# The unit of the largest and smallest expert on quarters of the partitions, with 32 slots of each

## The chip, the cores and the metric

The kernel runs on one core of a Trainium2 chip. The metric is the device time in microseconds; three runs of the kernel before gave 1936.6, 1944.35 and 1945.28 us.

## The reference, cut to what matters

A backbone of two layers over 256 latent tokens (and 256 context tokens) of width 1024, all in float32. Each layer is a mixer of four head groups and then a channel mixer: a dense SwiGLU in layer 0, and in layer 1, where only the latent tokens are left, eight experts of which each token uses two. The change lies in that last part:

```
def _swiglu(h, w_gate, w_up, w_down):
    return (jax.nn.silu(h @ w_gate) * (h @ w_up)) @ w_down
...
    top_val, top_idx = lax.top_k(logits, TOP_K)
    top_w = jax.nn.softmax(top_val, -1)
    gate = jnp.sum(jax.nn.one_hot(top_idx, N_EXPERTS, dtype=F32) * top_w[..., None], axis=-2)
    out = jnp.zeros(h.shape, F32)
    for e in range(N_EXPERTS):
        out = out + gate[..., e:e + 1] * _swiglu(h, w_gate[e], w_up[e], w_down[e]).astype(F32)
```

An expert has an inner width of 3584 (`D_FFE`) and three matrices of 1024 x 3584, so the eight together hold 352 MB, and each is read once. 256 tokens with two experts each fill 512 places.

## The kernel before, in words

Everything ahead of line 1404 (the parameters, both mixers, the dense SwiGLU, the routing logits) is the same in both kernels, apart from a few places where the scheduler swaps neighbours. `moe()` is the expert stage.

**Ranks, slots, units.** The experts are ranked by their number of tokens while the program runs; rank 0 has the most. `CAPS` gives each rank a number of slots (192 for rank 0, then 128, 128 and five times 64), `BASE` its first slot. 128 slots make a unit, one row of the partitions each. `UNITS` names the ranks of each unit: unit 0 holds 128 slots of rank 0, units 2 and 3 ranks 1 and 2, units 4 and 5 two ranks of 64 slots each, and unit 1 the last 64 slots of rank 0 beside the 64 of rank 7, the smallest. Units of one rank (0, 2, 3) are "whole". A token that finds no slot would be computed by `overflow`, a branch of which the body runs only if there is such a token.

**Two kinds of arithmetic.** A whole unit splits each half of a weight tile (ScalarE L1571, VectorE L1572) into two float32r parts, in `whl`, four buffers in turn, and multiplies each piece in three full-array matmuls (L1595, L1596, L1598). A unit of two ranks uses plain float32 (L1608): two matmuls of 64 array columns side by side, one on partitions 0 to 63 with one expert's weights, one on 64 to 127 with the other's, both over 512 moving columns. A float32 matmul is two instructions in the trace.

**Blocks and pairs.** The inner width goes in seven blocks of 512 (`NB`). In a block a rank has six weight pieces of 1 MB: gate 0 and 1, up 2 and 3, down 4 and 5; 48 pieces a block, 336 in all. They go into a ring of nine tiles (`mw`, line 1507; loads at L1660), in the order of first use; SyncE issues a load when the tile's last reader is done. The units are worked in pairs: `PAIRS` = (1, 0), (5, 2), (4, 3), that is with the ranks {0, 7}, {5, 6, 1} and {3, 4, 2}. Block 0 has the order (5), (4), (1, 0), (2, 3), with the gather of the tokens between; the last block has (1, 0), (5, 2), (3), (4). `swiglu_units` emits for a pair: gate of the first unit (8 k-steps), gate of the second, up of both, then Silu, product, transposes (L1630) and the down step (8 k-steps for two halves of 512 outputs) of each unit. `chain` keeps the matmuls in that order. The results are weighted and added into `yacc` by VectorE (L1744). After block 3 comes `overflow` (L1673), where all engines pass the branch and the loads in flight land first.

**The end.** After block 5 POOL multiplies each `yacc` by `gate`, a row broadcast to all partitions (`bcast_rows`, L431, at line 1755), and the last block's parts are multiplied by it on VectorE (L1747) before they are added (L1748). `combine` (L1713) sends each unit's `yacc` back to its tokens by a matmul with `DT`; unit 4's is L1771. A layer norm and the output follow.

Of the kernel before, what the change touches and what calls it, by code (L numbers as in the profile page):

```python
# [47 lines left out]
def _consts():  # L48
# [32 lines left out]
    put("iota", np.tile(np.arange(NSLOT), (P, 1)))  # L81
# [112 lines left out]
def kernel(ctx: ExitStack, tc: tile.TileContext, A, out: bass.AP):  # L194
# [1209 lines left out]
    def moe():  # L1404
# [108 lines left out]
        xg, yacc, gsl = {}, {}, tab(NU)  # L1513
        DT = mp.tile([P, NU, 256], F32R, name="DT")
        xgt = mp.tile([P, NU - len(WHOLE), KT, P], F32, name="xg")
        xhl = mp.tile([P, len(WHOLE), 2, KT, P], F32R, name="xhl")
        for u in range(NU):
            n = sum(v < u for v in WHOLE)
            xg[u] = (xhl[:, n, 0], xhl[:, n, 1]) if u in WHOLE else xgt[:, u - n]

        def gather(us):
# [35 lines left out]
            for j, u in enumerate(us):  # L1557
# [23 lines left out]
        def swiglu_units(units, nk):  # L1581
# [5 lines left out]
            def step(o, x, w, ws, a0, ks, nks, n=n):  # L1587

                if isinstance(x, tuple):
# [13 lines left out]
                for a, b, w_, pos_ in halves:  # L1603
# [13 lines left out]
            for i in range(2):  # L1617
                o2[i] = [ps("mm") for _ in units]
                for (xs, ws), o in zip(units, o2[i]):
                    for h in range(2):  # L1620
                        ms = step(o, xs, 2 * i + h, ws, 4 * h, range(4 * h, 4 * h + 4), KT)
                    chain[:] = ms
            ys = [[ps("mm" if u else "s5") for _ in range(2)] for u in range(len(units))]
            for u, (xs, ws) in enumerate(units):
                h = wtile("mh")[:, :n]
                S.activation(h, o2[0][u][:, :n], AF.Silu)  # L1626
                V.tensor_mul(h, h, o2[1][u][:, :n])  # L1627
                tp = ps("tr")
                for i in range(nk):
# [94 lines left out]
        for at, (b, us) in enumerate(order):  # L1724
# [155 lines left out]
```

## Time and profile before

| | us |
|---|---|
| median of three runs | 1944.35 |
| the profiled execution, its own time | 1943.62 |
| its span (first to last instruction) | 1941.8 |
| TensorE matmuls busy | 1810.1 |
| VectorE busy | 1071.2 |
| ScalarE busy | 693.1 |
| mean granted TensorE clock | 0.967 |

Times in the profile are in microseconds from the start of the span, unless marked ns. PE is TensorE's matmuls, PEld its weight loads, DVE VectorE, ACT ScalarE, POOL GpSimd, SP SyncE, which issues all DMAs. Spans of matmuls overlap, since their ends are modelled with the pipeline's depth; the distance between starts is what one costs. In a group of instructions the two numbers are the busy time of all and the mean of one in ns, then the idle time of the engine just before them with what ended it. The expert stage runs from about 1000 us to the end.

### The profile page before, as it was taken

Reading aid. Unit: us, or ns where it says so; the run is one execution under the profiler, and the core shown is the slowest. Engines: PE = TensorE matmul, PEld = TensorE weight load, DVE = VectorE, ACT = ScalarE, POOL = GpSimd, SP = SyncE. Lnnn points to the kernel's source line nnn. Section 1 sums busy time; section 2 is a strip of 40 time slices with the busy share of each in tenths; the row PEclk is TensorE's granted clock in tenths of the full one; section 3 lists DMA queues with packets and bytes.
Section 4 is the critical chain, followed back from the end, with each engine's and each line's share of the span. In section 5 each row is a group of like instructions: output and inputs, shape, how many; then the busy total and the mean of one; then the engine's idle time right before and its main releaser. Section 6 shows DMA issues by size and latency. Waiting matters only on the chain.

```text
span 1941.8 us, 23723 instructions
## 1 busy us (share of the span) xinstructions
PE 1810.1 (93%) x8634; PEld 1150.1 (59%) x8634; DVE 1071.2 (55%) x1715; ACT 693.1 (36%) x1077; POOL 420.8 (22%) x368
## 2 busy tenths in 40 slices
PE   6799989799999999899969999999999899999997
PEld 2576547778777777586654475554554454544553
DVE  7978544825456244849673383453543444554473
ACT  2245553422212222436623363342333333423340
POOL 3852232634342422522340000000000000021000
PEclk9899989899999999998979999999999999999999
DMA  8455831224534545251349987999999999999893
GB/s 315 151 164 195 290 133 65 102 95 144 187 133 165 177 172 190 76 188 52 122 164 371 417 333 324 423 420 407 422 400 422 369 379 421 409 398 421 349 378 133
DMA packets 111498, 508.57 MB, mean 262 GB/s; under 512 B 21776, under 2 KB 31632, under 8 KB 68368
## 3 DMA queue, kind: packets, MB, share of 16 engines
q1 hardware_dynamic: 111376, 507.01, 67.1%
q8 instruction: 69, 1.13, 0.2%
q14 instruction: 53, 0.43, 0.1%
HBM read 491.29 MB, written 15.66 MB: 261 GB/s over the span
## 4 chain that ended last, share of the span: by engine, by line
PE 79%; DVE 12%; DMA 3%; issue 2%; POOL 2%; ACT 1%; SPq 1%; DVEq 0%; POOLq 0%; ACTq 0%
PE ps L1608 24%; PE ps L283 8%; PE ps L284 8%; PE ps L285 8%; PE ps L1595 6%; PE ps L1598 6%; PE ps L1596 6%; PE ps L358 2%; PE ps L1096 1%; PE ps L1058 1%; PE ps L1057 1%; PE ps L1630 1%; DMA ring<-in_ada_w_dram 1%; PE ps L1114 1%; PE ps L1713 1%
## 5 line engine op out<-in xcount | busy, mean ns | idle before, releaser
L1572 DVE TENSOR_TENSOR whl<-ring,whl 128x1024 fp32r<-128x1024 f32 x252 | 307.3, 1254 | 114.3 <-ACT whl L1571 105.2
L1571 ACT ACTIVATE whl<-ring 128x1024 fp32r<-128x1024 f32 x252 | 258.0, 1054 | 234.9 <-PE ps L1596 128.8
L1608 PE MATMUL ps<-ring,xg 128*64 128x512 f32 x1344 | 302.2, 599 | 6.0 <-DMA ring<-in_moe_w_dram 6.0
L303 ACT ACTIVATE ring<-ring 128x1024 fp32r<-128x1024 f32 x114 | 120.0, 1059 | 312.7 <-PE ps L284 155.9
L283 PE MATMUL ps<-xa,ring 128*128 128x512 f32 (+1 forms) x576 | 217.2, 378 | 9.0 <-DVE xa L423 8.1
L285 PE MATMUL ps<-xa,ring 128*128 128x512 f32 (+1 forms) x576 | 216.7, 377 | 0.0
L284 PE MATMUL ps<-xb,ring 128*128 128x512 f32 (+1 forms) x576 | 216.2, 376 | 0.3 <-DVE xb L424 0.3
L1608 PEld LDWEIGHTS ps<-ring,xg 128*64 128x64 f32 x1344 | 94.6, 137 | 189.4 <-issue 186.4
L1750 POOL TENSOR_TENSOR yacc<-yacc,gate 128x1024 f32<-128x1024 f32 x6 | 21.1, 3512 | 766.9 <-DVE yacc L1744 734.9
L1608 PE MATMUL ps<-ring,mhT 128*64 128x512 f32 x672 | 161.8, 596 | 1.4 <-ACT mhT L1635 1.4
L305 DVE TENSOR_TENSOR ring<-ring,ring 128x1024 fp32r<-128x1024 f32 x76 | 106.0, 1397 | 90.9 <-ACT ring L303 90.5
L305 POOL TENSOR_TENSOR ring<-ring,ring 128x1024 fp32r<-128x1024 f32 x38 | 95.7, 2518 | 240.5 <-ACT ring L303 212.5
L1595 PE MATMUL ps<-whl,xhl 128*128 128x512 f32 x336 | 135.2, 402 | 0.0
L283 PEld LDWEIGHTS ps<-xa,ring 128*128 128x128 f32 x576 | 110.5, 192 | 36.1 <-DVE xa L423 8.5
L1596 PE MATMUL ps<-whl,xhl 128*128 128x512 f32 x336 | 131.2, 391 | 0.0
L1627 DVE TENSOR_TENSOR mh<-mh,ps 128x512 f32<-128x512 f32 x42 | 28.9, 687 | 185.3 <-PE ps L1608 159.9
L285 PEld LDWEIGHTS ps<-xa,ring 128*128 128x128 f32 x576 | 110.5, 192 | 24.4 <-issue 6.6
L284 PEld LDWEIGHTS ps<-xb,ring 128*128 128x128 f32 x576 | 110.3, 192 | 20.7 <-issue 2.8
L1598 PE MATMUL ps<-whl,xhl 128*128 128x512 f32 x336 | 104.2, 391 | 0.0
L1608 PEld LDWEIGHTS ps<-ring,mhT 128*64 128x64 f32 x672 | 48.4, 137 | 92.9 <-issue 90.6
L1744 DVE SCALAR_TENSOR_TENSOR yacc<-ps,mtab,yacc 128x512 f32<-128x512 f32 x60 | 45.0, 750 | 90.7 <-PE ps L1608 65.8
L1626 ACT ACTIVATE mh<-ps 128x512 f32<-128x512 f32 x42 | 25.0, 595 | 181.2 <-PE ps L1608 122.5
(445 smaller groups left out, 3026.6 us busy)
## 6 DMA issues: line engine op xcount, KB each, us to landing
ring<-in_moe_w_dram SPq DMA_DIRECT2D x334, 1024.0 KB, 10.5
ring<-in_ada_w_dram SPq DMA_DIRECT2D x96, 512.0 KB, 5.7
ring<-in_ffn_gu_dram SPq DMA_DIRECT2D x44, 512.0 KB, 3.5
ring<-in_w_in_dram SPq DMA_DIRECT2D x32, 512.0 KB, 4.7
ring<-in_ffn_d_dram SPq DMA_DIRECT2D x22, 512.0 KB, 3.8
ring<-in_w_out_dram SPq DMA_DIRECT2D x16, 512.0 KB, 3.9
s5CT<-CT SPq DMA_DIRECT2D x8, 512.0 KB, 3.4
s5WB<-WB SPq DMA_DIRECT2D x8, 512.0 KB, 3.0
```

Of the source, the lines that this page charges most:

```text
L283: PE.matmul(o, a[0], b[0], start=start, stop=False)
L284: PE.matmul(o, a[0], b[1], start=False, stop=False)
L285: PE.matmul(o, a[1], b[0], start=False, stop=stop)
L303: S.activation(hi, r, AF.Copy)
L305: (G if cnt[0] % 3 == 0 else V).tensor_sub(lo, r, hi.bitcast(F32))
L1571: S.activation(t[:, 0], src, AF.Copy)
L1572: V.tensor_sub(t[:, 1], src, t[:, 0].bitcast(F32))
L1595: PE.matmul(o[:, :n], xh[:, k], wh[:, k - k0], start=k == 0, stop=False)
L1596: PE.matmul(o[:, :n], xl[:, k], wh[:, k - k0], start=False, stop=False)
L1598: m = PE.matmul(o[:, :n], xh[:, k], wl[:, k - k0], start=False, stop=k == nks - 1)
L1608: PE.matmul(o[a:b, :n], x[:, k, a:b], w_(w)[:, k - a0], start=k == 0, stop=k == nks - 1, tile_position=pos_)
L1744: V.scalar_tensor_tensor(d, y[hf], g, d, op0=ALU.mult, op1=ALU.add)
```

## The change

Rank 0 gets 160 slots and rank 7 gets 32. Unit 1 now has four quarters of 32 partitions: the first two hold the same 32 slots of rank 0, the last two the same 32 slots of rank 7 (`SLOTS` repeats them, so that the gather puts each token there twice). The even quarter of an expert multiplies the first half of a weight piece's columns, the odd one the second half. A k-step is then four matmuls of 32 array columns and 256 moving columns, each at its own column position, where it was two of 64 and 512. The gate and up results of unit 1 are 256 wide, its `h` takes two transposes, and its `y` and `yacc` are 512 wide, with different output columns on even and odd quarters; so `DT` has a second version for it (`par` masks the even or the odd quarters), `combine` has two matmuls of 256 columns for it, and the gate row a rearranged copy, `gateq`. `gate` is made in the last block instead of early in the stage, POOL's products with it are gone, and the last block's parts are added first and multiplied after. `overflow` makes its own gate row, for which it passes five ring tiles over, not four. The hi and lo parts of the whole units' tokens get one tile each.

```
-CAPS = (192, 128, 128, 64, 64, 64, 64, 64)
-BASE = (0, 256, 384, 512, 576, 640, 704, 192)
+CAPS = (160, 128, 128, 64, 64, 64, 64, 32)
+BASE = (0, 256, 384, 512, 576, 640, 704, 160)
...
-UNITS = ((0, 0), (0, 7), (1, 1), (2, 2), (3, 4), (5, 6))
+UNITS = ((0, 0), (0, 0, 7, 7), (1, 1), (2, 2), (3, 4), (5, 6))
+NU = len(UNITS)
+QUART = {u for u, rk in enumerate(UNITS) if len(rk) == 4}
...
+SLOTS = np.arange(NU * P)
+SLOTS[P : 2 * P] = P + np.repeat([0, 0, 32, 32], 32) + np.tile(np.arange(32), 4)
...
+                if u in QUART:
+                    for i, v in enumerate((u, NU)):
+                        V.tensor_scalar(DT[:, v], tp[:, 0:256], C("par")[:, i : i + 1], None, op0=ALU.mult)
+                else:
+                    V.tensor_copy(DT[:, u], tp[:, 0:256])
...
-                halves = [(0, 128, ws[0], None)] if ws[0] is ws[1] else [
-                    (64 * a, 64 * a + 64, ws[a], (0, 64 * a)) for a in range(2)
-                ]
+                if len(ws) == 2 and ws[0] is ws[1]:
+                    parts = [(0, 128, ws[0], None, slice(0, n))]
+                else:
+                    z = 128 // len(ws)
+                    parts = [
+                        (z * a, z * a + z, w_, (0, z * a), slice(n * (a % 2), n * (a % 2) + n) if z == 32 else slice(0, n))
+                        for a, w_ in enumerate(ws)
+                    ]
...
                             PE.matmul(
-                                o[a:b, :n], x[:, k, a:b], w_(w)[:, k - a0], start=k == 0, stop=k == nks - 1, tile_position=pos_
+                                o[a:b, :n], x(k, a) if callable(x) else x[:, k, a:b], w_(w)[:, k - a0, c],
+                                start=k == 0, stop=k == nks - 1, tile_position=pos_,
                             )
-                            for a, b, w_, pos_ in halves
+                            for a, b, w_, pos_, c in parts
...
+                        for c, v, d in ((0, u, 256), (256, NU, 512)) if u in QUART else ((0, u, 512),):
+                            y = yacc[u][:, 256 * h : 256 * h + 256] if u in QUART else yacc[u][:, 512 * h : 512 * h + 512]
...
+            if (b, us) == (NB - 1, PAIRS[0]):
+                gate = mp.tile([P, D], F32, name="gate")
+                bcast_rows(gate, adaT[1][:, 40:48, 0])
+
+                gateq = mp.tile([P, 512], F32, name="gateq")
+                for a in range(4):
+                    r = slice(32 * a, 32 * a + 32)
+                    G.tensor_copy(
...
-                    elif b < NB - 1:
+                    else:
                         V.scalar_tensor_tensor(d, y[hf], g, d, op0=ALU.mult, op1=ALU.add)
-                    else:
-                        yg = wtile("mh")
-                        V.tensor_mul(yg, y[hf], gate[:, c])
-                        V.scalar_tensor_tensor(d, yg, g, d, op0=ALU.mult, op1=ALU.add)
-                if b == NB - 2:
-                    G.tensor_mul(yacc[u], yacc[u], gate)
+                    if b == NB - 1:
+                        V.tensor_mul(d, d, gt[:, c])
...
-                overflow([mw() for _ in range(4)])
+                overflow([mw() for _ in range(5)])
```

TensorE's row in block 1, at the transposes and the down step of pair (1, 0). `ring_7751` and so on are the weight tiles, `mh` and `mhT` unit 1's product and its transpose, `hTl` unit 0's. Before:

```order
L1598 MATMUL ps_8789<-whl_7761,xhl 128x512 x2
L1630 MATMUL ps_8848<-small,mh_7674 128x128 x4
L1608 MATMUL ps_8842<-ring_7751,mhT_7675 64x512
L1608 MATMUL ps_8842<-ring_7752,mhT_7675 64x512
...
L1608 MATMUL ps_8843<-ring_7753,mhT_7675 64x512
L1608 MATMUL ps_8843<-ring_7754,mhT_7675 64x512
...
L1630 MATMUL ps_8876<-small,mh_7673 128x128 x4
L1595 MATMUL ps_8844<-whl_7758,hTl_7763 128x512
```

The same place in the changed kernel, where "x2" joins the two quarters that read one weight tile:

```order
L1607 MATMUL ps_8839<-whl_7761,xhl_7766 128x512 x2
L1648 MATMUL ps_8913<-small,mh_7674 128x128 x2
L1622 MATMUL ps_8908<-ring_7751,mhT_7675 32x256 x2
L1622 MATMUL ps_8908<-ring_7752,mhT_7675 32x256 x2
...
L1648 MATMUL ps_8955<-small,mh_7673 128x128 x4
L1622 MATMUL ps_8908<-ring_7753,mhT_7675 32x256 x2
L1622 MATMUL ps_8908<-ring_7754,mhT_7675 32x256 x2
...
L1604 MATMUL ps_8909<-whl_7758,hTl_7763 128x512
```

Unit 1's matmuls stand where they stood, twice as many and a quarter of the size each; unit 0's transposes have moved ahead of unit 1's second down piece.

VectorE's row at the end of pair (1, 0) in the last block, before (`yacc_8070` is unit 1's, `yacc_8060` unit 0's):

```order
L1572 TENSOR_TENSOR hTl_7762<-ps_12784,hTl_7762 128x512
L1747 TENSOR_TENSOR mh_7674<-ps_12750,gate 128x512
L1748 SCALAR_TENSOR_TENSOR yacc_8070<-mh_7674,mtab,yacc_8070 128x512
L1747 TENSOR_TENSOR mh_7673<-ps_12751,gate 128x512
L1748 SCALAR_TENSOR_TENSOR yacc_8070<-mh_7673,mtab,yacc_8070 128x512
...
L1748 SCALAR_TENSOR_TENSOR yacc_8060<-mh_7673,mtab,yacc_8060 128x512
L1572 TENSOR_TENSOR whl_7758<-ring_7751,whl_7758 128x1024
```

And in the changed kernel, with `yacc_8073` for unit 1 and `yacc_8062` for unit 0:

```order
L1581 TENSOR_TENSOR hTl_7762<-ps_13089,hTl_7762 128x512
L1784 SCALAR_TENSOR_TENSOR yacc_8073<-ps_13042,mtab,yacc_8073 128x512
L1784 SCALAR_TENSOR_TENSOR yacc_8062<-ps_13043,mtab,yacc_8062 128x512
L1786 TENSOR_TENSOR yacc_8062<-yacc_8062,gate 128x512
...
L1786 TENSOR_TENSOR yacc_8073<-yacc_8073,gateq 128x512
L1581 TENSOR_TENSOR whl_7758<-ring_7752,whl_7758 128x1024
```

Unit 1's sum comes first, its product with `gateq` last, behind unit 0's, and the next pair's split of the weights stands behind that.

## Rows read from the trace of the kernel before

**Rows 1.** The page's first part: busy time, share of the span, instructions.

```profile
PE 1810.1 (93%) x8634; PEld 1150.1 (59%) x8634; DVE 1071.2 (55%) x1715; ACT 693.1 (36%) x1077; POOL 420.8 (22%) x368
```

**Rows 2.** Stretches: length, busy PE, PEld, DVE, ACT, POOL, then clock, DMA share, GB/s.

```profile
1002.00:1055.00 53.00, 46.18 (x248) 27.30 (x249) 26.04 (x90) 14.47 (x33) 3.25 (x3) 0.88 1.00 399
1055.00:1075.00 20.00, 18.43 (x101) 8.28 (x101) 7.21 (x20) 7.91 (x18) 0.00 (x0) 1.00 0.84 331
1110.00:1215.00 105.00, 102.22 (x454) 63.22 (x452) 60.73 (x61) 49.45 (x53) 0.00 (x0) 1.00 0.85 334
...
1510.00:1540.00 30.00, 24.01 (x96) 11.43 (x96) 14.38 (x15) 8.61 (x9) 0.00 (x0) 0.89 0.85 336
1550.00:1590.00 40.00, 39.66 (x180) 20.97 (x178) 15.75 (x17) 12.72 (x15) 0.00 (x0) 1.00 0.89 369
1590.00:1680.00 90.00, 86.52 (x379) 44.18 (x376) 43.05 (x43) 30.98 (x35) 0.00 (x0) 1.00 1.01 421
1680.00:1710.00 30.00, 29.66 (x135) 16.74 (x134) 15.72 (x14) 9.71 (x11) 5.67 (x2) 1.00 0.88 362
1710.00:1790.00 80.00, 73.19 (x317) 36.37 (x317) 42.72 (x38) 27.47 (x31) 11.99 (x4) 1.00 1.01 422
1790.00:1840.00 50.00, 49.66 (x224) 26.74 (x222) 23.02 (x25) 16.39 (x19) 3.41 (x1) 1.00 0.86 350
```

**Rows 3.** DMA issues, 1001 to 1935 us: count, KB each, median us to landing.

```profile
ring<-in_moe_w_dram SPq DMA_DIRECT2D x334, 1024.0 KB, 10.5
ring<-in_moe_w_dram SPq DMA_DIRECT2D x4, 512.0 KB, 7.0
fd<-ntab SPq DMA_DIRECT2D x2, 512.0 KB, 11.1
```

**Rows 4.** Timeline of SyncE: start, us, what; the first loads of the stage.

```profile
1001.68 8.63 SPq L1660 DMA_DIRECT2D ring<-in_moe_w_dram  x9
```

**Rows 5.** SyncE's longest wait in total, 1000 to 1942 us: us, times, longest.

```profile
SPq L1660 <- PE ps L1608: 448.1, 140, 10.4
```

**Rows 6.** The chain, 1155 to 1285 us: start, us, what; the pairs of block 1.

```profile
1159.22 7.02 PE ps L1608 x32
...
1200.24 7.02 PE ps L1608 x32
...
1280.82 4.43 PE ps L1608 x18
```

**Rows 7.** Timeline of PE: unit 1 and unit 2 begin in block 0.

```profile
1081.10 7.04 PE L1608 MATMUL ps<-ring,xg 128*64 128x512 f32 x32
...
1123.37 0.47 PE L1595 MATMUL ps<-whl,xhl 128*128 128x512 f32 x1
```

**Rows 8.** Timeline of PE: quarters of 32 columns, in both layers.

```profile
84.89 1.02 PE L709 MATMUL ps<-tabx,tabs 128*32 128x240 f32 x16
...
610.36 0.61 PE L709 MATMUL ps<-tabx,tabs 128*32 128x240 f32 x8
```

**Rows 9.** Groups by line, 1000 to 1942 us: busy us, mean ns, idle before.

```profile
L1608 PE MATMUL ps<-ring,xg 128*64 128x512 f32 x1344 | 302.2, 599 | 6.0 <-DMA ring<-in_moe_w_dram 6.0
L1608 PE MATMUL ps<-ring,mhT 128*64 128x512 f32 x672 | 161.8, 596 | 1.4 <-ACT mhT L1635 1.4
L1750 POOL TENSOR_TENSOR yacc<-yacc,gate 128x1024 f32<-128x1024 f32 x6 | 21.1, 3512 | 766.9 <-DVE yacc L1744 734.9 <-DMA ring<-in_moe_w_dram 32.0
L431 PE MATMUL ps<-small 128*128 128x128 f32 x16 | 2.4, 281 | 0.0
```

**Rows 10.** Timeline of PE: the first matmuls after the branch, their wait in brackets.

```profile
1532.80 3.68 PE L1608 MATMUL ps<-ring,xg 128*64 128x512 f32 x8 [5.99 <-DMA ring<-in_moe_w_dram]
```

**Rows 11.** Timeline of PE: unit 5's last down step, and what follows it.

```profile
1854.50 7.08 PE L1608 MATMUL ps<-ring,mhT 128*64 128x512 f32 x30
1862.46 0.47 PE L1595 MATMUL ps<-whl,hTl 128*128 128x512 f32 x1 [0.88 <-DVE mh L1747]
```

**Rows 12.** The 20 us around the wait of rows 10, columns as in rows 2.

```profile
1520.00:1540.00 20.00, 14.01 (x53) 7.07 (x52) 10.20 (x10) 4.51 (x5) 0.00 (x0) 0.83 0.97 374
```

More of the change, by code (lines that the diff above doesn't have):

```diff
@@ L1512, in moe @@
         iota = C("iota")
-        xg, yacc, gsl = {}, {}, tab(NU)
-        DT = mp.tile([P, NU, 256], F32R, name="DT")
+        xg, yacc, gsl, gate, gateq = {}, {}, tab(NU), None, None
+        DT = mp.tile([P, NU + 1, 256], F32R, name="DT")
         xgt = mp.tile([P, NU - len(WHOLE), KT, P], F32, name="xg")
-        xhl = mp.tile([P, len(WHOLE), 2, KT, P], F32R, name="xhl")
+        xhl = [mp.tile([P, 2, KT, P], F32R, name=nm("xhl")) for _ in WHOLE]
         for u in range(NU):
             n = sum(v < u for v in WHOLE)
-            xg[u] = (xhl[:, n, 0], xhl[:, n, 1]) if u in WHOLE else xgt[:, u - n]
+            xg[u] = (xhl[n][:, 0], xhl[n][:, 1]) if u in WHOLE else xgt[:, u - n]
         def gather(us):
@@ L1620, in swiglu_units @@
                     for h in range(2):
-                        ms = step(o, xs, 2 * i + h, ws, 4 * h, range(4 * h, 4 * h + 4), KT)
+                        ms = step(o, xs, 2 * i + h, ws, 4 * h, range(4 * h, 4 * h + 4), KT, 2 * n // len(ws))
                     chain[:] = ms
-            ys = [[ps("mm" if u else "s5") for _ in range(2)] for u in range(len(units))]
+            ys = [
+                [ps("mm" if u else "s5") for _ in range(4 // len(ws))] for u, (_, ws) in enumerate(units)
+            ]
             for u, (xs, ws) in enumerate(units):
-                h = wtile("mh")[:, :n]
-                S.activation(h, o2[0][u][:, :n], AF.Silu)
-                V.tensor_mul(h, h, o2[1][u][:, :n])
+                m = 2 * n // len(ws)
+                h = wtile("mh")[:, :m]
+                S.activation(h, o2[0][u][:, :m], AF.Silu)
+                V.tensor_mul(h, h, o2[1][u][:, :m])
                 tp = ps("tr")
-                for i in range(nk):
+                for i in range(m // 128):
                     PE.transpose(tp[:, 128 * i : 128 * i + 128], h[:, 128 * i : 128 * i + 128], ident)
@@ L1707, in combine @@
         def combine(units):
+            units = sorted(units, key=lambda u: u in QUART)
             for h in range(2):
@@ L1712, in combine @@
                     for u in units:
-                        PE.matmul(
-                            o, DT[:, u, 128 * t : 128 * t + 128].bitcast(F32), yacc[u][:, 512 * h : 512 * h + 512],
-                            start=u == units[0], stop=u == units[-1],
-                        )
+                        for c, v, d in ((0, u, 256), (256, NU, 512)) if u in QUART else ((0, u, 512),):
+                            y = yacc[u][:, 256 * h : 256 * h + 256] if u in QUART else yacc[u][:, 512 * h : 512 * h + 512]
+                            PE.matmul(
+                                o[:, c:d], DT[:, v, 128 * t : 128 * t + 128].bitcast(F32), y,
+                                start=u == units[0], stop=u == units[-1] and d == 512,
+                            )
                     z = res[t + 2][:, 512 * h : 512 * h + 512]
```

37 lines of the change are left out of this document (21 added, 16 removed).

## The prediction

> **What bounds the kernel now.** The page's first part comes first: TensorE is busy for 93% of the span [rows 1]. That alone says "PE-bound", and would make every PE saving a saving of time, so the next view is the busy time by stretch of the expert stage, for the column GB/s and not for PE [rows 2]. It runs at 421 GB/s with a DMA share of 1.01 for stretches of 80 and 90 us; no row passes 422. 338 loads bring 336 tiles of 1 MB, 352.3 MB [rows 3], and at 421 GB/s these alone take 837 us, from the first issue at 1001.7 us [rows 4] to 1838.5 us at best. So the stage has two limits that lie close together. Between the full stretches are short ones of 362, 369, 350 or 334 GB/s, in which PE is busy for 97 to 99% [rows 2]. What happens in those is in SyncE's waits: it stands 140 times, 448 us in all, in front of a ring tile that L1608 still reads [rows 5].
>
> A tile costs the DMA 1.0486 MB / 421 GB/s = 2.49 us. Pair (1,0) reads two experts, 12 tiles, 29.9 us; pairs (5,2) and (4,3) read three, 18 tiles, 44.8 us. On PE the three cost about the same: the chain has unit 1 of block 1 beginning at 1159.2, the next pair at 1200.2 and block 2 at 1280.8 [rows 6], so 41.0 us for (1,0) and 40.3 us for each other pair. In (1,0) PE is 11 us slower than the loads, the nine-tile ring fills and the loads stop; in the other two PE is 4.5 us faster each and comes to wait for tiles. A block takes 121.6 us there, 119.6 us of it being the time of its 48 tiles: the two limits take turns, and neither hides the other whole.
>
> **The change, part by part.** *Quarters.* A k-step of unit 1 is now two half-array matmuls of 512 columns; 8 steps take 7.04 us [rows 7], 0.88 us each. It becomes four of 32 array columns and 256 moving columns. The nearest row is L709, four quarters of 240 columns: 16 instructions in 1.02 us, 8 in 0.61 us [rows 8], so 0.205 us for four; for 256 columns 0.219 us, and a step (two instructions to a float32 matmul) 0.44 us. With 24 steps a block this saves 24 x 0.44 = 10.6 us a block, 74 us of the 302 + 162 us of L1608 [rows 9]. Bounds: nothing saved (quarters one after another in pairs) up to the 10.6 us.
>
> The same row bears on a rule that speaks against the change. L709 keeps four quarters side by side at the price of one. The Trainium skill (TensorE: Matmul & The Clock Gate, Measured speedup vs the span model) reports 2.38-fold for three column tiles of 32. By that rate, an estimate from that page, four would give 3.2-fold, a step 0.55 us, a saving of 8 us a block and an end some 2 us later; the trace does not agree, and I go by L709.
>
> *What that does to a block.* Pair (1,0) falls from 41.0 to 30.4 us, level with its 29.9 us of loads, and no pair is slower on PE than on the DMA any more: 111 us a block against 119.6. So from here the loads set the pace, and most of the 74 us turns into waiting on PE. What is left to win is what the loads lose now.
>
> A second rule would leave nothing to win. The rows show 421 GB/s [rows 2]. The Trainium skill (DMA: Bandwidth & Descriptors, Where 436 GB/s comes from) puts a core's HBM loads at about 358 GB/s; by that the 352.3 MB would take 984 us, longer than the stage is. The trace disagrees, so the rule has no share in the sum.
>
> *The loads' lost time.* Lost is length x (1 - rate/421), by [rows 2]. At the start 53 x (1 - 399/421) = 2.8 and 20 x (1 - 331/421) = 4.3 us: gathers and unit 5, unchanged, kept. From 1110 to 1215, 21.7 us: pairs (1,0) and (2,3) of block 0 and (1,0) of block 1 take 42.3, 35.8 and 41.0 us on PE [rows 6, 7] against 29.9 each, an excess of 29 us of which the ring swallows some 7. After it the excess is 42.3 - 10.6 - 2.4 (L431 of line 1755, which moves away [rows 9]) - 29.9 = -0.6, then 5.9, then 0.5: 6 us, which the ring can swallow; I keep 3 (bounds 0 and 6). At line 1673 the loads drain, 30 x (1 - 336/421) = 6.1 us, and PE stands idle for 6 us [rows 2, 10]: kept, with one more ring tile passed over. The branch itself stays untaken: the reference's own router on its inputs gives the experts 137, 103, 67, 59, 44, 43, 39 and 20 tokens, within 160 and 32. At (1,0) in blocks 4, 5 and 6: 4.9, 4.2 and 8.4 us, gone.
>
> *The rest.* Unit 1's Silu, product, transposes and accumulate halve, and a second D costs one product in the gather: none is on the path. The gate's broadcast (2.4 us of PE) now lies in the last block's pair (1,0), where PE waits for loads. POOL loses six products of 3.5 us [rows 9] and gets four copies for gateq, each at most half of such a product, 7 us in all at most; their user, VectorE's product on unit 1's yacc, stands behind unit 0's down matmuls of some 6 us in its queue. I take 0, and 1 us as the upper bound; the next pair's splits are queued behind it. In combine, two matmuls of 256 columns replace one of 512: 0. VectorE's two operations for each half of y change places: 0.
>
> **The sum.** The end hangs on unit 5's down step in the last block, since from its end at 1861.6 us to the span's end at 1941.8 PE has work without a pause over 0.9 us, apart from the closing normalization [rows 11]: 80.2 us, kept. That step needs tile 316 of 336. Tiles: 316 x 1.0486 + 1.05 MB (the tokens spilled for the overflow [rows 3]) = 332.4 MB, at 421 GB/s 789.6 us. First issue 1001.7 + 789.6 + losses 7.1 + 3 + 6.1 = 1807.5 us; the tile's own matmuls 3.5 us: 1811.0 us. With the tail 1891.2 us. I add 2 us for waits on PE after which its clock is granted at half (below): span 1893. The profiled run's time is 1943.6 for a span of 1941.8, 1.8 more, and lies 0.7 below the median of 1944.35. So **1895 us**, 2.5% less. Of 74 us saved on PE, some 49 us arrive. Bounds: no loss in block 0 and no added 2 us, 1890, and 1883 if the 7.1 us at the start went too; above, 6 us in block 0, 1 us for gateq and 3 us lost at each of five pairs (1,0), since the ring holds tiles that PE lags behind on, 1914.
>
> **Rivals.** *The ring still fills at (1,0).* PE ends a pair some 6 us after its last tile, and a tile is held until split and multiplied; if that lag keeps the loads waiting for half of what they lose now (half of 21.7 + 17.5, 20 us), 1915 us. For: in blocks 4 to 6 the stalls are there though PE waits for tiles elsewhere. Against: stretches of 80 and 90 us without any stall, with the same lag [rows 2].
>
> *Quarters run in pairs.* Then the change doesn't do what it says: PE as before, plus what the broadcast adds, 1944 us. For: nothing in the expert stage. Against: L709.
>
> *PE alone sets the pace.* Then all 74 us arrive: 1870 us. Against: 837 us of loads, and no row over 422 GB/s.
>
> *The clock falls, slower than before.* PE will wait for tiles in every block. After the 6 us that it stood at the branch the granted clock of the 20 us there was 0.83 [rows 10, 12]: a drop from 2.4 to 1.2 GHz, with 6.8 us at the lower level (0.17 x 20 x 2), which costs 3.4 us of PE work. PE's reserve is 119.6 - 111 = 8.6 us a block; up to two drops a block cost little, and it decides against the change from some five a block (17 us, 8.4 over the reserve, 59 us in seven blocks). With eight: 1895 + 7 x (27.2 - 8.6) = 2025 us. Against: I find one wait of about 3.3 us a block, when unit 1 has used its first two tiles and the next two land 5 us later, and stretches with PE at 92% keep a clock of 1.00 (the last but one of [rows 2]).
>
> **How the numbers follow.** Forecast 1895: 0.83. Ring 1915: 0.07. Pairs 1944: 0.04. PE alone 1870: 0.02. Clock 2025: 0.04. The range of 1882 to 1918 covers the forecast's bounds and the ring, and leaves out some 0.1 to 0.15. A measurement of this kernel tells 0.5% (10 us) from no change: faster by more 0.92, within 0.04, slower 0.04.
>
> **What will show it.** Unit 1's eight k-steps in 3.5 us, not 7.0, with four starts together: the quarters. Pair (1,0) at about 30 us, a block at 119 to 121 us, 420 GB/s through 1110 to 1800 but for the branch, SyncE's waits on L1608 far shorter and PE's on tiles or splits longer: the loads as the pace. A granted clock under 1.00 within blocks would speak for the last rival; rates under 400 GB/s at (1,0) for the first. Wrong it is if the block stays at 122 us or more, or if the tail after unit 5's last down step is not about 80 us.

## The result, and the profile after

The changed kernel takes **1891.22 us** (median; 1889.33 to 1896.53), the kernel before, timed beside it, 1944.16 us: a ratio of 0.974, 95% interval 0.9709 to 0.9772. That is 2.7% less; 1895 was predicted, 1882 to 1918. The profiled execution took 1891.42 us for a span of 1889.6 us.

The page's first part, as [rows 1], shows almost nothing of it. TensorE is as busy as before, 93%:

```profile
PE 1748.1 (93%) x9300; PEld 1146.3 (61%) x9300; DVE 1055.4 (56%) x1708; ACT 687.5 (36%) x1076; POOL 402.7 (21%) x366
```

The stretches of the expert stage do show it (columns as in [rows 2]; the first two are of the same lengths as there, counted from this trace's own first load at 997.8 us). Between 1110 and 1800 us the last column is the same everywhere except around the branch: the short rows of 334, 369, 362 and 350 GB/s are gone from the blocks. Only the last row, in the last block, shows the loads held up by the ring's readers again.

```profile
998.00:1051.00 53.00, 45.96 (x269) 28.42 (x269) 28.24 (x96) 16.64 (x38) 3.48 (x3) 0.90 0.99 402
1051.00:1071.00 20.00, 18.43 (x92) 6.73 (x93) 5.53 (x16) 6.31 (x14) 0.00 (x0) 1.00 0.95 369
1110.00:1215.00 105.00, 101.39 (x592) 65.59 (x592) 64.08 (x65) 48.96 (x55) 0.00 (x0) 1.00 1.01 421
1215.00:1475.00 260.00, 247.32 (x1336) 136.59 (x1333) 119.65 (x119) 93.04 (x107) 0.00 (x0) 0.99 1.01 421
1475.00:1510.00 35.00, 26.12 (x148) 13.84 (x147) 15.88 (x17) 10.13 (x13) 0.00 (x0) 0.85 0.85 347
1510.00:1590.00 80.00, 78.59 (x442) 44.75 (x442) 37.11 (x37) 28.91 (x33) 0.00 (x0) 1.00 1.01 421
...
1710.00:1790.00 80.00, 75.53 (x472) 43.99 (x470) 39.02 (x40) 29.19 (x34) 2.43 (x4) 1.00 1.01 421
...
1810.00:1850.00 40.00, 38.70 (x149) 26.00 (x149) 30.64 (x34) 13.70 (x14) 0.00 (x0) 1.00 0.85 350
```

PE's timeline gives the pairs, answering [rows 6, 7, 11] (L1622 is the old L1608). The lines are the first matmuls of: (1,0), (5,2) and (4,3) of block 1, block 2, block 3, block 6; then, in block 6, unit 1's wait for a tile, its up step, and last unit 5's last down step.

```profile
1141.58 3.66 PE L1622 MATMUL ps<-ring,xg 128*32 128x256 f32 x64
...
1170.87 1.51 PE L1622 MATMUL ps<-ring,xg 128*64 128x512 f32 x6
...
1212.97 1.51 PE L1622 MATMUL ps<-ring,xg 128*64 128x512 f32 x6
...
1253.96 2.41 PE L1622 MATMUL ps<-ring,xg 128*32 128x256 f32 x36
...
1372.55 1.98 PE L1622 MATMUL ps<-ring,xg 128*32 128x256 f32 x32
...
1739.34 2.35 PE L1622 MATMUL ps<-ring,xg 128*32 128x256 f32 x36
1743.20 1.92 PE L1622 MATMUL ps<-ring,xg 128*32 128x256 f32 x28 [1.50 <-DMA ring<-in_moe_w_dram]
1750.72 4.34 PE L1622 MATMUL ps<-ring,xg 128*32 128x256 f32 x64
...
1801.37 7.08 PE L1622 MATMUL ps<-ring,mhT 128*64 128x512 f32 x30
```

The first line is the quarters: 64 instructions, eight k-steps, in 3.66 us, against 7.02 for 32 half-array instructions; the starts of four quarters lie within 0.02 us of each other. Pair (1,0) falls from 41.0 to 29.3 us. Block 1 takes 112.4 us, PE's own length (the loads had gained a lead by then: tile 50, the block's second, landed at 1132.5 us, 9 us before its first matmul); block 2 takes 118.6 us, about the loads' length.

The groups by line, 1000 to 1890 us, as [rows 9]; the last two are the copies for gateq and the late broadcast:

```profile
L1622 PE MATMUL ps<-ring,xg 128*64 128x512 f32 (+1 forms) x1792 | 270.4, 498 | 19.5 <-DMA ring<-in_moe_w_dram 17.0 <-issue 2.2
L1622 PE MATMUL ps<-ring,mhT 128*64 128x512 f32 (+1 forms) x896 | 138.7, 489 | 3.5 <-ACT mhT L1653 3.5
...
L1772 POOL COPY gateq<-gate 32x512 f32<-32x512 f32 x4 | 2.4, 607 | 765.6 <-ACT gate L440 765.5
L436 PE MATMUL ps<-small 128*128 128x128 f32 x16 | 2.2, 281 | 0.0
```

Busy time in L1622 fell by 31.8 + 23.1 = 55 us, not 74: part of the waiting counts as busy. Eight k-steps of quarters take 4.34 us at 1750.72, not 3.66, and no idle time is marked in them. Idle time on tiles rose from 6.0 to 17.0 us.

The waits, 1000 to 1890 us (engine, line, released by: us, times, longest), as [rows 5]; SyncE's two, then ScalarE's splits, which waited 88.6 us, 24 times, before:

```profile
SPq L1684 <- PE ps L1622: 352.7, 136, 12.2
SPq L1684 <- DVE whl L1581: 232.6, 111, 4.8
...
ACT whl L1580 <- DMA ring<-in_moe_w_dram: 234.0, 60, 12.5
```

And the DMA issues, as [rows 3]:

```profile
ring<-in_moe_w_dram SPq DMA_DIRECT2D x334, 1024.0 KB, 15.8
```

From issue to landing now takes 15.8 us, not 10.5. At 2.49 us a tile that is some six tiles in the queue: SyncE still stands in front of a ring tile, but the DMA behind it has work. SyncE's wait is therefore no sign of a lost load; the GB/s column is.

### The profile page after: what moved, and what is told of

It is laid out like the page before. It is cut to its first block, busy times and chain, and to the rows that moved or that the text cites. A ratio compares the mean times of both kernels' runs of the same rounds, so it can differ in the third digit from the quotient of the medians.

```text
span 1889.6 us, 24989 instructions
## 1 busy us (share of the span) xinstructions
PE 1748.1 (93%) x9300; PEld 1146.3 (61%) x9300; DVE 1055.4 (56%) x1708; ACT 687.5 (36%) x1076; POOL 402.7 (21%) x366
## 4 chain that ended last, share of the span: by engine, by line
PE 71%; DVE 13%; DMA 12%; issue 2%; ACT 2%; POOL 1%; SPq 0%; DVEq 0%; ACTq 0%; POOLq 0%
PE ps L1622 16%; DMA ring<-in_moe_w_dram 11%; PE ps L288 9%; PE ps L290 9%; PE ps L289 9%; PE ps L1604 5%; PE ps L1607 5%; PE ps L1605 5%; PE ps L363 3%; PE ps L1063 1%; PE ps L1062 1%; PE ps L1101 1%; PE ps L1119 1%; DVE ring L310 1%; PE ps L1648 1%
## 5 line engine op out<-in xcount | busy, mean ns | idle before, releaser
L1581 DVE TENSOR_TENSOR whl<-ring,whl 128x1024 fp32r<-128x1024 f32 x252 | 299.1, 1221 | 165.4 <-ACT whl L1580 156.3
L1622 PE MATMUL ps<-ring,xg 128*64 128x512 f32 (+1 forms) x1792 | 270.4, 498 | 19.5 <-DMA ring<-in_moe_w_dram 17.0
L288 PE MATMUL ps<-xa,ring 128*128 128x512 f32 (+1 forms) x576 | 217.0, 378 | 10.5 <-DVE xa L428 8.2
L1622 PEld LDWEIGHTS ps<-ring,xg 128*64 128x64 f32 (+1 forms) x1792 | 96.7, 125 | 174.4 <-issue 132.7
L1622 PE MATMUL ps<-ring,mhT 128*64 128x512 f32 (+1 forms) x896 | 138.7, 489 | 3.5 <-ACT mhT L1653 3.5
L1784 DVE SCALAR_TENSOR_TENSOR yacc<-ps,mtab,yacc 128x512 f32<-128x512 f32 x66 | 49.5, 750 | 93.6 <-PE ps L1622 60.9
L1645 DVE TENSOR_TENSOR mh<-mh,ps 128x512 f32<-128x512 f32 (+1 forms) x42 | 27.0, 642 | 131.2 <-PE ps L1622 106.4
L1622 PEld LDWEIGHTS ps<-ring,mhT 128*64 128x64 f32 (+1 forms) x896 | 46.7, 123 | 76.2 <-issue 61.4
L363 PE MATMUL ps<-ring,small 128*32 128x512 f32 x384 | 74.4, 665 | 12.3 <-ACT small L340 6.5
## 6 DMA issues: line engine op xcount, KB each, us to landing
ring<-in_moe_w_dram SPq DMA_DIRECT2D x334, 1024.0 KB, 15.8
```

Source lines behind the costliest of these rows:

```text
L288: PE.matmul(o, a[0], b[0], start=start, stop=False)
L363: PE.matmul(o[32 * j : 32 * j + 32, :], act[:, k, :], w[:, i, :], start=h < 2, stop=h >= 2, tile_position=(0, 32 * j),)
L1581: V.tensor_sub(t[:, 1], src, t[:, 0].bitcast(F32))
L1622: PE.matmul(o[a:b, :n], x(k, a) if callable(x) else x[:, k, a:b], w_(w)[:, k - a0, c], start=k == 0, stop=k == nks - 1, tile_position=pos_,)
```

## Where the 52 us came from

Three marks divide each trace: the first load's issue (I), the first matmul of block 1 (B1) and of block 6 (B6), and the span's end. The table gives I and then the three lengths, all from the timelines of the profiled executions, with the median time beside them. The experiments that keep the order of the pairs in blocks 0 to 5 stand in it too, and are told below. Differences in the text are of unrounded times.

| kernel | I | I to B1 | B1 to B6 | B6 to end | time, median |
|---|---|---|---|---|---|
| before | 1001.7 | 157.5 | 627.6 | 155.1 | 1944.2 |
| after | 997.8 | 143.8 | 597.8 | 150.3 | 1891.2 |
| before_half1 | 1004.1 | 146.8 | 601.0 | 145.7 | 1899.6 |
| before_half5 | 1005.4 | 151.5 | 609.2 | 148.2 | 1909.8 |
| after_half5 | 1002.6 | 141.5 | 599.5 | 147.2 | 1892.9 |
| before_gate | 1003.2 | 154.4 | 623.2 | 157.0 | 1938.3 |
| before_less | 996.0 | 152.1 | 620.7 | 152.5 | 1926.2 |
| after_less | 1001.9 | 139.5 | 574.5 | 150.2 | 1866.8 |
| after_ring7 | 1000.6 | 150.2 | 603.4 | 153.1 | 1905.3 |
| after_last | 1005.5 | 144.4 | 597.3 | 156.3 | 1905.2 |

Of the 52.2 us between the two spans, 3.8 lie ahead of the first load, 13.7 before block 1, 29.8 in blocks 1 to 5 and 4.8 in the last block. The 3.8 us can't be put down to the change: I lies between 996.0 and 1005.4 in the traces of the kernel before and its four variants here, and between 997.8 and 1005.5 in those of after and its four. That is a spread of some 10 us with the same work ahead of it; how much of it belongs to the execution and how much to the order in which a build puts that work is open. The lengths behind I are the surer measure.

## The experiments

**Is PE's time in unit 1 enough?** before_half1 takes only unit 1's columns, no quarters (`cut` is set for unit 1 alone):

```diff
                 for k in ks:
+                    c = slice(0, 256 if cut and k else n)
                     with behind(*chain):
...
-                                o[a:b, :n], x[:, k, a:b], w_(w)[:, k - a0], start=k == 0, ...
+                                o[a:b, c], x[:, k, a:b], w_(w)[:, k - a0, c], start=k == 0, ...
```

> The kernel before, with only half of unit 1's matmuls in time: every k-step of unit 1 but the first of its chain multiplies 256 of the 512 columns (left out: the other 256 columns of these k-steps, and with them the right numbers of unit 1). No quarters, no moved gate, no other tables. Saved on PE: 20 of 24 k-steps of a block, 0.44 us each, 8.8 us a block, 62 us in seven blocks; pair (1,0) falls from 41.0 to 32.2 us against 29.9 us of loads, the block from 121.6 to 112.8 us on PE against 119.6 us of loads. Theory (the loads set the pace as soon as (1,0) no longer lags): blocks of 119 to 121 us, rates of 420 GB/s through (1,0), time 1893 to 1903 us, close to the changed kernel's 1891 although PE has 12 us more to do. Rival 1 (PE sets the pace): 1944 - 62 = 1882 us. Rival 2 (the quarters as such, or the moved gate, bring the gain): above 1915 us.

Measured 1899.58 us, ratio 0.9781 (0.9755 to 0.9807). The theory's range holds it, and neither rival's does. From B1 to B6 it needs 601.0 us against after's 597.8, with 1.8 us a block more for PE: quarters as such aren't needed, only less time on PE. The profiled run began its loads 6.2 us later than after's, which is most of the 8 us between the two spans.

**Does the place matter?** before_half5 is the same cut with unit 5 in place of unit 1.

> The kernel before, with the same 8.8 us a block taken from unit 5 in pair (5,2) instead of unit 1 in (1,0): every k-step of unit 5 but the first of its chain multiplies 256 of 512 columns (left out: the other 256 columns of them). PE has as little to do as in the run that halves unit 1, but (1,0) still takes 41.0 us against 29.9 us of loads, while (5,2) falls to some 31.5 us against 44.8. Theory (it matters where PE is slower than the loads): the ring swallows some 7 us of the 11 us that PE falls behind in (1,0) and the loads stop for the other 4: blocks of 122 to 125 us, time 1910 to 1930 us. Rival (only the sums of a block count, 112.8 us of PE against 119.6 of loads): 1893 to 1903 us, as with unit 1 halved.

Measured 1909.81 us, ratio 0.9832 (0.9805 to 0.9858): 0.2 us below the theory's range, 7 above the rival's. But the stretches divide it (columns as in [rows 2]). First before_half5:

```profile
1060.00:1115.00 55.00, 49.92 (x223) 23.43 (x219) 19.08 (x19) 15.74 (x18) 0.00 (x0) 1.00 1.01 422
1115.00:1232.00 117.00, 112.41 (x534) 74.77 (x534) 73.16 (x73) 57.12 (x61) 0.00 (x0) 1.00 0.88 351
1232.00:1400.00 168.00, 160.35 (x722) 88.06 (x718) 78.63 (x80) 60.51 (x68) 0.00 (x0) 1.00 1.01 421
```

and before_half1 in the same stretches:

```profile
1060.00:1115.00 55.00, 53.08 (x283) 29.54 (x280) 25.26 (x30) 22.72 (x31) 0.00 (x0) 1.00 0.99 406
1115.00:1232.00 117.00, 113.56 (x542) 72.41 (x541) 72.17 (x72) 55.36 (x61) 0.00 (x0) 1.00 0.99 406
1232.00:1400.00 168.00, 161.61 (x763) 93.06 (x762) 83.30 (x83) 63.55 (x71) 0.00 (x0) 1.00 1.01 421
```

The difference is in 1115 to 1232 us, a loss of 117 x (1 - 351/421) = 19.5 us against 4.2, where (2,3) of block 0 and (1,0) of block 1 follow one another. (4,3) of block 1 and all of block 2 lie in the third stretch, (1,0) with its 41 us among them, and nothing is lost: **the ring swallows the whole 11 us of one (1,0)** when PE came to it without a backlog. I had said 7, and my theory of a loss in every block falls. From there on before_half5 keeps 420 GB/s (1400 to 1490 us) and 417 (1540 to 1765): in the later blocks it is nearly the sums of a block alone that count.

**A pair with more loads in between.** before_half5_order takes block 1 as (5,2), (1,0), (4,3):

```diff
-        order = {0: ((5,), (4,), (1, 0), (2, 3)), NB - 1: ...}
+        order = {0: ((5,), (4,), (1, 0), (2, 3)), 1: (PAIRS[1], PAIRS[0], PAIRS[2]), NB - 1: ...}
```

> The kernel before with unit 5 halved as in the run with 1909.8 us (left out: 256 of 512 columns of each of its k-steps but a chain's first), and block 1 in the order (5,2), (1,0), (4,3). In that run the loads lost 19 us between 1115 and 1232 us, in (2,3) of block 0, (1,0) of block 1 and the pair behind it, and next to nothing in the later (1,0). Theory (three pairs with more PE than loads stand in a row there, 12 + 6 + 11 us of excess against one ring; a pair with more loads between them takes the loss away): some 10 us of the 19 come back, 1896 to 1905 us. Rival (the loss belongs to each first use, not to the row of pairs): 1906 to 1914 us.

Measured 1908.55 us, ratio 0.9826 (0.9809 to 0.9844): no gain that can be told, and in the rival's range. The stretches show why the numbers don't settle it:

```profile
1115.00:1232.00 117.00, 112.73 (x535) 74.27 (x536) 73.95 (x74) 60.53 (x65) 0.00 (x0) 1.00 0.96 389
1232.00:1350.00 118.00, 114.28 (x544) 63.31 (x540) 56.43 (x57) 39.00 (x45) 0.00 (x0) 1.00 0.98 402
```

The first stretch did get back 10 of its 19 us (117 x (1 - 389/421) = 8.9 left). But I had overlooked that the moved (1,0) now stands close to the next one, with one full (4,3) between them, and the second stretch loses 5.3 us that before_half5 didn't lose. That pairs in a row add up agrees with both; that spacing them helps the time isn't shown.

**Is after still bound by PE?** after_half5 makes the same cut in the changed kernel's unit 5.

> The changed kernel, with unit 5's k-steps but the first of each chain cut to 256 of 512 columns as well (left out: the other 256 columns of them): PE loses another 8.8 us a block, 62 us in all, and has 102 us of work in a block against 119.6 us of loads. Theory (the loads set the pace): blocks stay at 118 to 121 us, time 1886 to 1893 us, at most 5 us less; PE waits for tiles some 60 us more. Rival 1 (PE sets the pace): 1891 - 62 = 1829 us. Rival 2 (longer waits lower the granted clock): above 1897 us, with stretches of a granted clock below 1.00 in several blocks.

Measured 1892.93 us, ratio 0.9747 (0.9722 to 0.9772), at the upper end of the theory's range and 64 us away from the rival's. 62 us of PE work less bring nothing: B1 to B6 takes 599.5 us against 597.8. Its stretches:

```profile
1215.00:1475.00 260.00, 233.68 (x1315) 139.25 (x1314) 117.19 (x117) 91.15 (x104) 0.00 (x0) 0.99 1.01 421
1550.00:1800.00 250.00, 225.68 (x1320) 137.12 (x1319) 118.64 (x120) 90.65 (x104) 2.43 (x4) 1.00 1.01 421
1170.00:1190.00 20.00, 18.27 (x98) 12.13 (x98) 6.13 (x6) 6.23 (x8) 0.00 (x0) 0.91 1.01 420
1290.00:1310.00 20.00, 16.94 (x94) 10.76 (x90) 6.22 (x6) 7.00 (x9) 0.00 (x0) 0.91 1.01 422
1540.00:1560.00 20.00, 17.37 (x97) 11.84 (x92) 8.64 (x8) 9.48 (x11) 0.00 (x0) 0.91 1.01 422
```

The same 421 GB/s, with PE busy for 90%. The sign of the second rival is there, but not its price: the granted clock falls in three blocks (the last three rows, 0.91 over 20 us, once each in blocks 1, 2 and 4), and the loads go on at 420 to 422 GB/s meanwhile. 0.09 x 20 = 1.8 us of PE work lost each time fit into the 17 us a block by which PE is shorter than the loads here.

**Fewer loads.** Both kernels with 14 tiles not fetched:

```diff
             def load(rs, i):
+                if rs == [6] and i in (1, 3):
+                    ws[6].append(ws[6][i - 1])
+                    return
```

> The kernel before with 14 of its 336 tiles not loaded: in each block the second half of the gate piece and of the up piece of one expert of unit 5 (pair (5,2)) is not fetched, its first half is used again (left out: those two quarters of that expert's weights). The loads of a block fall from 119.6 to 114.6 us, PE's work stays at 121.6. Theory (before, PE is the slower one over a block and the ring stops the loads): 1935 to 1944 us. Rival (the loads were the pace already before): 1944 - 14 x 2.49 = 1909 us.

> The changed kernel with the same 14 tiles not loaded (left out: those two quarters of one expert's weights; their first halves are used twice). The loads of a block fall from 119.6 to 114.6 us, PE's work stays at 111. Theory (the loads set the pace): unit 5's last down step ends 14 x 2.49 = 35 us earlier, the 81 us behind it stay: 1853 to 1862 us. Rival (PE sets the pace): within 3 us of 1891.

before_less: 1926.18 us, ratio 0.9926 (0.9897 to 0.9955), between theory and rival. after_less: 1866.84 us, ratio 0.9614 (0.9585 to 0.9643), 24 us less than after, far from the PE rival and short of the theory's 29 to 38. The table tells both. In after_less, B1 to B6 shrinks by 23.3 us; ten tiles were left out there, 10 x 2.49 = 24.9 us. But its last block takes the 150.2 us that it took before, though two more tiles are missing in it. **Blocks 1 to 5 are the loads'; in the last block fewer loads bring nothing.** In before_less the blocks shrink by 6.9 us and the part before them by 5.4: the loads had a small share in the pace of before as well. By PE's timeline blocks 2, 4 and 5 of the kernel before take 123.2, 125.8 and 128.1 us, more than PE's 121.6 and more than the loads' 119.6; I had taken block 1 for all of them.

**The gate alone.** before_gate moves the broadcast, drops POOL's products, changes VectorE's order and gives the branch its fifth tile:

```diff
+            if (b, us) == (NB - 1, PAIRS[0]):
+                gate = mp.tile([P, D], F32, name="gate")
+                bcast_rows(gate, adaT[1][:, 40:48, 0])
...
-                if b == NB - 2:
-                    G.tensor_mul(yacc[u], yacc[u], gate)
```

> The kernel before, with the other part of the change alone: the gate is made in the last block's pair (1,0) rather than in block 0, POOL's six products with yacc go, VectorE's two operations change places in the last block, and the overflow branch takes a fifth ring tile. Units and slots as before; nothing left out. Theory (this part is worth nothing by itself): 1940 to 1945 us, the 2.4 us of PE saved in block 0's (1,0) being all it can bring there. Rival (a good share of the 53 us comes from it): below 1930 us.

Measured 1938.26 us, ratio 0.9983 (0.9971 to 0.9994): 3 us less than before, 2 below the theory's range, nowhere near 53.

**The ring.** after_ring7 has `NRAW = 7` for 9.

> The changed kernel with a ring of seven tiles rather than nine, nothing left out. It tells whether the lead that the ring stores still matters: PE's pairs now need 30, 40 and 40 us against 30, 45 and 45 of loads, so no pair falls behind the loads by more than the tiles in hand. Theory (no lead is needed any more): 1889 to 1900 us, seven tiles being 17 us of loads. Rival (tiles are held by PE so long that the ring's depth sets the rate): 1910 us or more, with rates of 400 GB/s or less at every pair.

Measured 1905.26 us, ratio 0.9805 (0.9778 to 0.9833), between the two: 14 us more than after. The two spans are 17.7 us apart, of which the table puts 2.8 ahead of the first load, 6.5 before block 1, 5.7 into blocks 1 to 5 and 2.8 into the last block. The rates:

```profile
1001.00:1054.00 53.00, 46.17 (x249) 27.69 (x250) 28.08 (x95) 15.71 (x36) 3.27 (x3) 0.88 0.92 358
1003.00:1200.00 197.00, 185.15 (x1154) 114.70 (x1154) 107.17 (x182) 83.39 (x118) 1.35 (x2) 0.96 0.97 392
1200.00:1480.00 280.00, 264.96 (x1408) 149.03 (x1406) 130.83 (x131) 97.77 (x111) 0.00 (x0) 1.00 1.01 420
1540.00:1800.00 260.00, 248.24 (x1350) 139.71 (x1339) 120.99 (x123) 90.52 (x103) 2.43 (x4) 1.00 1.01 419
```

Seven tiles are enough for the pairs of the blocks from 1200 us on (420 and 419 GB/s), not for the start. There the largest part of the loss, 53 x (402 - 358)/421 = 5.5 us, lies in the first 53 us, with the gathers and unit 5; 2.8 us more are lost between 1151 and 1200 us (397 GB/s), in the first pairs of block 1.

**Can the last block be shortened?** after_last turns its order:

```diff
-        order = {..., NB - 1: (PAIRS[0], PAIRS[1], (3,), (4,))}
+        order = {..., NB - 1: (PAIRS[1], PAIRS[2], PAIRS[0])}
```

> The changed kernel with the last block in another order, (5,2), (4,3), (1,0) rather than (1,0), (5,2), unit 3, unit 4; the gate is made at the last block's first pair and the closing sum takes units 1 and 0. Nothing left out. If the loads set the pace, the 81 us of PE work behind unit 5's last down step are what can still be hidden: the whole-expert units, which need much PE for each tile, then run while the loads go on, the loads end without a stall at about 997.8 + 336 x 2.49 + 2.5 (spill) + 6 (start) + 6 (branch) = 1849 us, and some 25 us of work on the last tiles, the closing sums and the normalization follow. Theory: 1868 to 1882 us. Rival (PE sets the pace): within 5 us of 1891.

Measured 1905.18 us, ratio 0.9812 (0.9786 to 0.9838): slower than after, outside both. Its last block, split where the loads end:

```profile
1747.00:1862.00 115.00, 109.72 (x549) 59.18 (x548) 56.25 (x61) 40.10 (x45) 2.42 (x4) 0.99 1.01 417
1862.00:1903.00 41.00, 31.25 (x157) 18.76 (x155) 21.76 (x31) 6.50 (x9) 2.53 (x2) 0.92 0.09 35
```

The loads do run through, as wanted, and then 41 us of work are left, in PE's timeline (1,0)'s down steps and the closing sums of (4,3):

```profile
1866.05 2.35 PE L1622 MATMUL ps<-ring,mhT 128*32 128x256 f32 x36 [0.47 <-ACT mhT L1653]
1868.92 1.92 PE L1622 MATMUL ps<-ring,mhT 128*32 128x256 f32 x28
1871.33 5.31 PE L1742 MATMUL ps<-yacc,DT 128*128 128x512 f32 x12
```

6 us of the 14 are the longer last block (156.3 against 150.3), 7.7 the later I. My 1849 us for the loads' end took after's I of 997.8; the last tile landed at 1862.1, 13 us later, of which the later I explains 7.7. And 41 us of work followed, not 25.

**Moving the last block's PE work to the middle.** after_spread puts the last block's steps of units 2 and 3 behind blocks 2 and 3; a unit's closing sum follows its last step.

```diff
-        order = {..., NB - 1: (PAIRS[0], PAIRS[1], (3,), (4,))}
+        order = {..., NB - 1: (PAIRS[0], (5,), (4,))}
         order = [(b, us) for b in range(NB) for us in order.get(b, PAIRS)]
+        for u, b in ((2, 2), (3, 3)):
+            order.insert(order.index((b, PAIRS[-1])) + 1, (NB - 1, (u,)))
+        fin = {u: at for at, (_, us) in enumerate(order) for u in us}
...
-                    if b == NB - 1:
+                    if at == fin[u]:
                         V.tensor_mul(d, d, gt[:, c])
```

> The changed kernel with the last block's steps of units 2 and 3 (a whole expert each: some 20 us of PE for 15 us of loads) put behind blocks 2 and 3, so that the last block is (1,0), unit 5, unit 4, and the closing sums of units 2 and 3 fall into blocks 5 and 6. Nothing left out. From the last block's first matmul the changed kernel needs 150 us in each of its forms so far (1739.3 to 1889.6), because PE has more to do there than the loads; in blocks 2 to 5 it waits for tiles. Theory (PE's surplus of the last block fits into those waits): the loads run at 420 GB/s until the last tile lands at 1001 + 336 x 2.49 + 2.5 + 12 = 1852 us (5 us either way with the stage's start), 3.5 us of matmuls and the closing 13.3 us follow: 1866 to 1880 us. Rival 1 (PE has no room for it in the middle, the ring fills there): 1889 to 1896 us, as the changed kernel. Rival 2: the wider spacing of PE's work lowers the clock or breaks a row of loads: above 1896.

Measured 1886.99 us, ratio 0.9707 (0.9693 to 0.9721): below the first rival's range and above the theory's, 4 us less than after. The same shift in before_gate's kernel, before_gate_spread:

> The kernel before with the late gate (1938.3 us), and in it the same shift of the last block's units 2 and 3 to places behind blocks 2 and 3. Nothing left out. There PE has 121.6 us of work in a block against 119.6 of loads, no room in the middle. Theory (the shift pays only where the loads set the pace): 1932 to 1942 us. Rival (the shift shortens the end whatever sets the pace): 1915 to 1925 us, as much as it gains in the changed kernel.

Measured 1946.47 us, ratio 1.0013 (1.0003 to 1.0024), 8 us more than before_gate (6 by the two ratios) and 4 above the range: where PE is full, the shift brought nothing and rather cost. Last, after_spread2 also moves (1,0) of the last block between (5,2) and (4,3) of block 5:

```diff
-        order = {..., NB - 1: (PAIRS[0], (5,), (4,))}
+        order = {..., NB - 1: ((5,), (4,))}
...
+        order.insert(order.index((NB - 2, PAIRS[1])) + 1, (NB - 1, PAIRS[0]))
```

> As the shifted changed kernel (1886.99 us), and besides (1,0) of the last block stands between (5,2) and (4,3) of block 5, so that the last two steps are unit 5 and unit 4 alone, 60 us of loads for some 40 us of PE, and the closing sum of units 1 and 0 is done before them. Nothing left out. In that run the loads went on at 420 GB/s to about 1858 us and 28 us passed from there to the end, 9 of them because PE was still in unit 4's up step when the last tile landed. Theory (what is left of the end is PE's lag, and it goes when the last loads have less PE work beside them): 1874 to 1882 us, some 19 us from the last tile to the end. Rival (PE is as busy as the loads through the whole stage, so a shift only moves the lag): 1884 to 1892 us.

Measured 1885.51 us, ratio 0.970 (0.968 to 0.9721): the rival's. PE's timeline at its end:

```profile
1845.21 3.70 PE L1742 MATMUL ps<-yacc,DT 128*128 128x512 f32 x8
1848.74 1.02 PE L1803 MATMUL ps<-small 128*128 128x512 f32 x2
1849.69 3.65 PE L1622 MATMUL ps<-ring,xg 128*64 128x512 f32 x14
1853.27 2.84 PE L1803 MATMUL ps<-small 128*128 128x512 f32 x6
1856.05 3.65 PE L1622 MATMUL ps<-ring,xg 128*64 128x512 f32 x16
1861.90 7.09 PE L1622 MATMUL ps<-ring,mhT 128*64 128x512 f32 x32 [0.69 <-ACT mhT L1653]
1868.92 3.70 PE L1807 MATMUL ps<-yacc,DT 128*128 128x512 f32 x8
```

The last tile landed at 1856.6 us, and PE is still in unit 4's up step. The two shifted kernels are the fastest of those that leave nothing out, by 4 and 6 us against after: their executions (1883.34 to 1888.06 and 1884.11 to 1886.44) all lie below after's lowest, but against the spread of I that is little, and the intervals of the ratios overlap.

## Why the prediction was right

- **Quarters.** 0.44 us a k-step predicted, 3.66/8 = 0.46 measured; all four run side by side, as their starts show. The estimate from the Trainium skill (TensorE: Matmul & The Clock Gate, Measured speedup vs the span model), 0.55 us, is too high here.
- **The loads become the pace.** Shown for blocks 1 to 5: 597.8, 599.5, 597.3 and 601.0 us in four kernels whose PE work there differs by up to 53 us, and 574.5 us with ten tiles fewer. Five blocks of loads are 598 us; that after hits this figure so closely is partly luck, since 7 us of lead used up in block 1 make up for 8 at the branch. Within a block PE waits for unit 1's fourth tile: in block 2 until 1258.23 us (tile 100 landed at 1258.19), in block 3 until 1377.57 (tile 148 at 1377.52), in block 6 until 1743.20 (tile 292 at 1743.15). No row passes 422 GB/s, and long ones stand at 421. The Trainium skill (DMA: Bandwidth & Descriptors, Where 436 GB/s comes from) gives 358 GB/s as the limit of a core, half of what two cores share; the loads of the one core that runs here pass it.
- **Pair and block.** 30.4 us predicted for (1,0), 29.3 measured where PE doesn't wait; blocks 2, 4 and 5 take 118.6, 118.6 and 120.7 us, 119 to 121 predicted. Of the kernel before, 121.6 us was block 1 alone; its blocks 2, 4 and 5 take 2 to 7 us more.
- **Lost time of the loads.** Start: 7.1 us "kept", 53 x (1 - 402/421) + 20 x (1 - 369/421) = 4.9 measured. Block 0: 3 taken, 0 measured. Branch: 6.1 taken, 35 x (1 - 347/421) = 6.2 measured. Later (1,0): gone, as predicted.
- **The step that failed** is the path at the end: "that step needs tile 316 of 336", with "the tile's own matmuls 3.5 us" behind it. Tile 316 landed at 1802.8 us (tile 317, 2.49 us behind it, lets ScalarE's split start at 1805.37), 4.7 us before the predicted 1807.5: the first load came 3.9 earlier and some 5 us of the losses didn't occur; against that the sum's 332.4 MB had moved at 1799.2, 3.6 us before the tile was whole, since parts of the tiles behind it were among them. But the step ended at 1808.45, 5.6 us behind the tile, because it wasn't the tile that held it. PE's last marked wait for a tile is the 1.50 us up to 1743.20, for tile 292. From there to 1808.45 PE works for 65 us with one marked pause, 0.56 us for VectorE's product in (1,0). I had the loads as the pace until tile 316; in the last block they were it for its first four tiles. The gate's broadcast, which I took at 0 because PE would wait there, stands in that row of work with its 2.2 us, and (1,0) takes 34.6 us there against 29.9 of loads. So it is partly luck that the sum came out: 4.7 us too late for the tile and 2.1 too little behind it gave 1811.0 for 1808.45. From there PE has work to the end, 81.2 us (80.2 predicted). That fewer loads don't shorten the last block, its 150 us in after_less show; that tile 316 is close behind, after_half5 shows, where 8.8 us of PE work less shorten it by 3.1 only.

```profile
1761.55 0.66 PE L1648 MATMUL ps<-small,mh 128*128 128x128 f32 x4 [0.56 <-DVE mh L1645]
1762.04 1.06 PE L436 MATMUL ps<-small 128*128 128x128 f32 x8
1805.37 2.01 ACT L1580 ACTIVATE whl<-ring 128x1024 fp32r<-128x1024 f32 x2 [3.30 <-DMA ring<-in_moe_w_dram]
```

- **The clock.** 2 us taken; a drop within the blocks happened once. From 1370 to 1390 us the granted clock is 0.91, 0.09 x 20 x 2 = 3.6 us at 1.2 GHz, at the waits of 0.57 and 1.85 us within (1,0) of block 3. Such a stretch costs 1.8 us of PE work; the loads keep 421 GB/s through it, so nothing of it shows in the time.
- **Gate and POOL.** 0 to 1 us taken; gateq's copies are 2.4 us on an engine with nothing else to do, and before_gate shows 3 us of gain for this part. In these traces the gain lies ahead of the last block: that block itself takes 157.0 us in before_gate against 155.1, and 145.7 in before_half1, which leaves the gate where it was, against after's 150.3.
- **SyncE's waits** were to be "far shorter"; they fell from 448 to 353 us only. That was the wrong sign to watch, as told above.

What stays open: how much of before's 123 to 128 us a block was which limit (before_less fits neither side's numbers), and whether another order gets below 1885 us.

## What to carry to other kernels

When an engine is 93% busy and the transfers are within some per cent of their rate, look at the rate by stretch, and at sums by block of both: work taken from the busy engine pays until the other limit is reached, here some 48 of 74 us, and then not at all. A ring evens out a pair that falls behind by less than it holds, so where in a block the saving lies matters little in the steady part, and much where several such pairs follow each other at the start. Check the last block on its own: closing sums and other work that stands only there can make another engine the late one. A rate from summed bytes isn't the landing of a tile either: look for the last wait on a tile before you let the end hang on one.

## What the runs showed of the hardware

- Loads of 1 MB ran at 421 GB/s for some 360 us on end (1110 to 1475), with PE, VectorE and ScalarE busy for 95, 46 and 36% beside them (the row from 1215 us).
- PE busy for 90%, the rest in short waits, kept a mean granted clock of 0.99 to 1.00 (after_half5), where I had feared a drop with each wait. It did fall in blocks 1, 2 and 4, to 0.91 over 20 us each, at no cost in time. In after it fell at the 6.65 us wait at the branch (0.85 over 35 us) and at the 1.85 us one in block 3.
- Four matmuls on quarters of 32 columns with 256 moving columns each, float32, took 0.46 us a k-step of two instructions each, half of the 0.88 us of two halves with 512: the four run at once, each on its own moving data.
- The time at which the stage's first load is issued varies by some 10 us between traces of kernels that do the same work until there, more than several of the effects looked for.
